# A decoder step whose late stages do their element-wise work on DVE alone, and whose epilogues write over the values they are given

## The chip, the cores and the metric

The kernel runs on one core of a Trainium2 chip. The metric is the device time of one execution in microseconds. Three runs of the kernel before took 1580.48, 1581.73 and 1584.48 us, the median is 1581.73 us.

Five engines work side by side: PE multiplies matrices, DVE (VectorE), ACT (ScalarE) and POOL (GpSimd) do element-wise work, and the queue of SP issues all the DMAs that are spoken of here. Each engine takes its instructions strictly in the order that is written for it; one that waits holds up all that stand behind it. All of POOL's work in this kernel has its operands in SBUF.

## The reference, cut to what matters

One layer: a wide input projection, two branches (a gated recurrence A and windowed attention B), each projected back, a merge with sigmoid gates, an output projection, a norm and a gated embedding that is added.

```python
    u = rmsnorm(x, norm_pre)
    proj = jnp.einsum('bld,de->ble', u, w_in)
    aq, af, ai, aog, az, bq, bk, bv, bz, ga, gb = jnp.split(proj, offs, axis=-1)
    ...
    oa = (oa * jax.nn.silu(az.astype(jnp.float32))).astype(x.dtype)
    a = jnp.einsum('ble,ed->bld', oa, w_pa)
    ...
    b = jnp.einsum('ble,ed->bld', ob, w_pb)
    m = jax.nn.sigmoid(ga) * a + jax.nn.sigmoid(gb) * b
    y = jnp.einsum('bld,de->ble', m, w_o)
    x = x + rmsnorm(y, norm_post)
    e = jnp.einsum('blp,pd->bld', pl, w_ple) * jax.nn.sigmoid(jnp.einsum('bld,de->ble', x, w_ple_gate))
    x = x + e
```

There are 1024 prompt tokens and 32 sample tokens (1056 columns), the model is 1024 wide, everything is float32.

## The kernel before, in words

Values lie transposed: 128 channels in the partitions, tokens in the columns, eight tiles of 128 x 1056 for a 1024-wide value. Each float32 operand of a matmul is split into a high part (`H..`, `wh`) and a low part (`L..`, `wl` = value - high); a product is three matmuls, high x high, high x low, low x high.

**A pair.** `pair_gemm` makes two output tiles (two times 128 channels) at once, with a Strassen-like scheme over the first three of each four k-tiles: seven products P1, P5, P6, P3, P7, P2, P4 (nine matmuls of 512 columns each), each of which takes one combination of weights (`prep`, lines 288 to 316: sums `ws` at L296 and L309, the high part at L285, the low part at L286) and one variant of the values (B11, T1, T2, B22, T3, B21, T4). The remaining k-tiles ("R") are done plainly, four times six matmuls, after P6, P3, P2 and P4. The 32 sample columns are done apart, on `gs`, after P1. Three PSUM banks go round; the outputs leave them through DVE: `p` at L492, and the three `out` sums of L448 in the order u (after P3), p (after P7) and c (after P2); the fourth output is read by the epilogue from PSUM. P2 needs the bank that L492 has read, P4 the bank that the sum with p has read.

**The late stages**, four pairs each: the second gate (`gate_b`, pairs 0 to 3, of which 2 and 3 are "late"), projection A (`pa`), projection B with the merge (`pb`), the output projection (`o`), then the small embedding projection `ple` with the residual beside it, and its gate. The values of a stage are made from the outputs of the stage before by `build`: 12 differences (L1481), 25 high parts by ACT (L1469, L1483) and 25 low parts (L1470, L1484). A variant can be rebuilt only when the last pair of the stage before has used it, so `build` runs along the last pair of one stage and the first pair of the next, in the order B11, T1, T2, B22, R, T3, B21, T4. The epilogues of `pb` and `o` do not begin before the whole of `build` has been written down.

**Who does what.** Before, POOL makes the sums `ws`, the low parts of P1, P2 and P4, the low parts of B11 and of every second tile of the others, one of the merge additions (L1545), and in the residual (`residual`, lines 1604 to 1664) half of the multiplications by the norm's factor (L1648) and half of the low parts (L1662). DVE does the rest.

**Order.** PE's order is the order in which the code is written: the generators (`build`, `turn_p`, `residual`) are stepped by `tick()` every three matmuls in the late stages, and what they emit stands there. The order of the other engines is made by a scheduler when the kernel is built. A tile pool hands out a buffer when its former user is done with it: `ct`, three buffers of 128 x 512, is used by `out`, the epilogues, T3 and T4 of `build` and by `turn_p`; `t12` is one buffer, which `build` holds for `ts` until the last low part of T4, if it uses it for that.

`turn_p` (L1562) loads nine pieces of the layer's embedding (L1566), turns each by two transposes on PE (`ppp`, L1570) and splits it into `pH` and `pL` for `ple`.

Of the kernel before, what the change touches and what calls it, by code (L numbers as in the profile page):

```python
# [11 lines left out]
F32 = mybir.dt.float32  # L12
# [4 lines left out]
ALU = mybir.AluOpType  # L17
# [3 lines left out]
P = 128  # L21
# [6 lines left out]
M = 3  # L28
# [93 lines left out]
def tile_decoder_step(ctx: ExitStack, tc: tile.TileContext, x_prompt, x_sample, state_hgrn, cache_k, cache_v,  # L122
# [70 lines left out]
    def enqueue(gen, delay=1, q=0):  # L193
        queues[q].append([gen, delay])
# [94 lines left out]
    def prep(W):  # L289

        a11, a21, a12, a22 = (W.raw[i][:, 0:M, j, :] for i in range(2) for j in range(2))
        shape = [P, M, P]

        def sums(a, b, op):
            s = wp.tile(shape, F32, name=tname("ws"), tag="ws", bufs=2)
            G.tensor_tensor(s, a, b, op=op)  # L296
            return s

        split(W, "P1", a11, G, shape, "w", 4)
        yield  # L300
# [8 lines left out]
        G.tensor_tensor(s2, a12, s2, op=ALU.subtract)  # L309
        split(W, "P3", s2, V, shape, "w", 4)  # L310
        yield
        split(W, "P7", s3, V, shape, "w", 4)
        yield
        split(W, "P2", a12, G, shape, "w", 4)
        yield
        split(W, "P4", a22, G, shape, "w", 4)
        yield

    def prep_plain(W):

        shape = [P, M, P]
        for n, (i, j) in enumerate(((0, 0), (1, 0), (0, 1), (1, 1))):
            split(W, (i, j), W.raw[i][:, 0:M, j, :], G if n % 2 else V, shape, "w", 4)
            if n == 1:
                rest(W)
            yield
# [6 lines left out]
    def rest(W):  # L333
        if R:
# [468 lines left out]
    def hgrn_proj(h, pairs, pre=()):  # L803
# [615 lines left out]
    def gate_b(p, late=False):  # L1419
        def ep_gb(i):  # L1420
            def ep_(ci, sl, ps):
                sg = ctile()[:, :ps.shape[-1]]
                S.activation(sg, ps, AF.Tanh, scale=0.5)
                V.tensor_scalar(sg, sg, 0.5, 0.5, op0=ALU.mult, op1=ALU.add)
                DM.dma_start(gb_d[i][:, sl], sg)
            return ep_

        pair_gemm(gb_pairs[p], u, (ep_gb(2 * p), ep_gb(2 * p + 1)), quantum=3 if late else A_QUANTUM, late=late)
# [25 lines left out]
    def build(x, prev, src):  # L1454

        ts = rt.tile([P, M, HT], F32, name=tname("ts"), tag="t12")
        for n in ("B11", "T1", "T2", "B22", "R", "T3", "B21", "T4"):
            yield until(("used", id(prev), n))
            if n == "B22":
                sample_side(x)  # L1460
                for i in range(KT):
                    V.tensor_copy(x.s[:, i, :], src[i][:, ssl])
                x.made.add("s")
            if n == "R":
                for sl in (H0, H1):
                    for kt in range(KT):
                        if kt % 4 >= M:
                            h, l = block(x, kt, sl.start, sl.stop)
                            S.copy(h, src[kt][:, sl])  # L1469
                            (V if kt < 4 else G).tensor_tensor(l, src[kt][:, sl], h, op=ALU.subtract)  # L1470
                            yield B_WAIT
                x.made.add(n)
                continue
            for i in range(M):
                a, b = src[i], src[4 + i]
                s = {"B11": a[:, H1], "B22": b[:, H0], "B21": b[:, H1], "T1": ts[:, i], "T2": ts[:, i]}.get(n)
                if s is None:
                    s = ctile()
                if n[0] == "T":
                    p, q = {"T1": (a[:, H0], a[:, H1]), "T2": (b[:, H0], s), "T3": (b[:, H0], a[:, H0]), "T4": (b[:, H1], ts[:, i])}[n]  # L1480
                    V.tensor_tensor(s, p, q, op=ALU.subtract)  # L1481
                h, l = (v[:, i] for v in x.v[n])
                S.copy(h, s)  # L1483
                (G if i == 1 or n == "B11" else V).tensor_tensor(l, s, h, op=ALU.subtract)  # L1484
# [49 lines left out]
    def eps_pb(i):  # L1534
        gbt = gl.tile([P, NTOK], F32, name=f"gbr{i}", tag=f"gl{i // 4}", bufs=2)
        DM.dma_start(gbt, gb_d[i])

        def ep_(ci, sl, ps):
            if ms[i] is None:
                while ("built", id(xb)) not in done:  # L1540
                    tick()
                ms[i] = staged(i, "m")
                DM.dma_start(ms[i], ma_d[i])
            V.tensor_tensor(gbt[:, sl], gbt[:, sl], ps, op=ALU.mult)
            (G if ci == HT else V).tensor_tensor(ms[i][:, sl], ms[i][:, sl], gbt[:, sl], op=ALU.add)  # L1545
# [14 lines left out]
    yT = [None] * KT  # L1560

    def turn_p():  # L1562
        for i in range(9):
            r = P if i < 8 else 32
            pt = ctile()[:, :256]
            DM.dma_start(pt[:r], p_prompt[0, 0, i * P:(i + 1) * P, :] if i < 8 else p_sample[0].rearrange("b t d -> (b t) d"))  # L1566
            yield 4
            b = fps.tile([P, 512], F32, name=f"ppp{i}", tag="xp", bufs=3)
# [27 lines left out]
    small = rt.tile([P, M * HT], F32, name="small", tag="t12")  # L1596
# [8 lines left out]
    def residual():  # L1605
# [39 lines left out]
                S.copy(rb_[:, lo:lo + w], b[:, :w])  # L1645
        yield 2
        for n, i in enumerate(order):
            (G if n % 2 else V).tensor_tensor(yT[i], yT[i], rb_, op=ALU.mult)  # L1648
            for hf in range(3):
                m, r = (4, P) if hf < 2 else (1, 32)  # L1650
                b = fps.tile([P, 512], F32, name=f"xtp{i}_{hf}", tag="xp", bufs=3)
# [3 lines left out]
                V.tensor_tensor(yT[i][:, sl], yT[i][:, sl], b[:, :sl.stop - sl.start], op=ALU.add)  # L1655
# [89 lines left out]
```

## Time and profile before

| | |
|---|---|
| runs | 1580.48, 1581.73, 1584.48 us |
| the profiled execution, own time | 1583.84 us |
| its span, first to last instruction | 1581.9 us |
| mean granted PE clock | 0.983 |
| late stages in it (from the third pair of the second gate) | 1081.9 us to the end |

The page gives the busy time of each engine over the span. The late stages are read pair by pair: a pair of seven products has the same 107 matmul instructions everywhere, so that a pair that waits for nothing shows what PE needs for it, and the length of the others what they lose. The order of time on one engine shows, in brackets, how long the engine stood idle before an instruction and what ended that; a row with "x2" is two instructions back to back.

### The profile page before, as it was taken

How to read it: one execution, taken by the hardware profiler on the slowest of the kernel's cores; microseconds unless marked ns; L12 is line 12 of the kernel's file. 1: busy time of each engine (PE TensorE's matmuls, PEld its weight loads, DVE VectorE, ACT ScalarE, POOL GpSimd, SP SyncE). 2: the span in 40 equal slices, each digit the busy share in tenths (PEclk: the TensorE clock that was granted, in tenths of full speed). 3: DMA queues.
4: the chain of work that ended last, by engine and by line, in shares of the span. 5: the costliest groups of instructions: out<-in, count | busy, mean ns of one | idle time of the engine just before them, and what ended most of it. 6: DMA issues, size and time to landing. Idle time of an engine off the chain costs nothing.

```text
span 1581.9 us, 27515 instructions
## 1 busy us (share of the span) xinstructions
PE 1499.7 (95%) x10013; PEld 1180.4 (75%) x10013; DVE 1053.3 (67%) x2240; ACT 729.8 (46%) x1881; POOL 630.1 (40%) x550
## 2 busy tenths in 40 slices
PE   8888999999999999999899999999999997998998
PEld 8767787878777777787677776777777775788776
DVE  7666858584858585763677777744957879547432
ACT  6234444445353545445555565543624433545422
POOL 1355444535354444455222222232736556224200
PEclk9999999999999999999999999999999998999999
DMA  5212131212121212213112111135463631223221
GB/s 182 67 30 81 41 97 41 73 52 82 55 83 55 77 60 63 75 50 94 40 48 51 47 48 51 56 113 206 147 210 122 214 100 35 60 62 93 80 80 55
DMA packets 198003, 129.54 MB, mean 82 GB/s; under 512 B 47075, under 2 KB 185500, under 8 KB 197852
## 3 DMA queue, kind: packets, MB, share of 16 engines
q1 hardware_dynamic: 197052, 127.54, 26.6%
q8 instruction: 79, 1.29, 0.3%
q14 instruction: 56, 0.46, 0.1%
q0 software_dynamic: 672, 0.18, 0.1%
q10 hardware_dynamic: 144, 0.07, 0.0%
HBM read 96.89 MB, written 31.88 MB: 81 GB/s over the span
## 4 chain that ended last, share of the span: by engine, by line
PE 66%; DVE 22%; issue 4%; ACT 3%; DMA 3%; POOL 2%; SPq 0%; DVEq 0%; ACTq 0%; POOLq 0%
PE g L404 47%; PE gs L386 3%; DVE ct L448 2%; PE po L1259 2%; DVE QE L938 2%; PE pt L1244 1%; PE g L835 1%; DVE wl L286 1%; DVE LT L1484 1%; PE gs L394 1%; PE d L1053 1%; PE lp L1212 1%; DVE stk L1397 1%; PE d L1055 1%; PE d L1015 1%
## 5 line engine op out<-in xcount | busy, mean ns | idle before, releaser
L286 POOL TENSOR_TENSOR wl<-raw,wh 128x384 fp32r<-128x384 f32 x150 | 169.6, 1134 | 359.5 <-ACT wh L285 345.5
L404 PE MATMUL g<-HT,wh 128*128 128x512 f32 x588 | 242.7, 413 | 16.7 <-DVE ct L448 12.9
L404 PE MATMUL g<-LT,wh 128*128 128x512 f32 x588 | 234.0, 398 | 0.9 <-POOL LT L1484 0.9
L404 PE MATMUL g<-HT,wl 128*128 128x512 f32 x588 | 234.4, 399 | 0.0
L404 PE MATMUL g<-HB,wh 128*128 128x512 f32 x522 | 214.6, 411 | 7.1 <-ACT p L441 5.2
L404 PE MATMUL g<-HB,wl 128*128 128x512 f32 x522 | 206.2, 395 | 0.0
L404 PE MATMUL g<-LB,wh 128*128 128x512 f32 x522 | 205.9, 395 | 0.0
L285 ACT CAST wh<-ws 128x384 fp32r<-128x384 f32 x184 | 93.8, 511 | 175.4 <-PE g L404 114.0
L404 PE MATMUL g<-HR,wrh 128*128 128x512 f32 x416 | 174.0, 418 | 0.0
L404 PE MATMUL g<-HR,wrl 128*128 128x512 f32 x416 | 166.0, 399 | 0.0
L286 DVE TENSOR_TENSOR wl<-ws,wh 128x384 fp32r<-128x384 f32 x184 | 128.6, 700 | 55.7 <-ACT wh L285 54.4
L404 PE MATMUL g<-LR,wrh 128*128 128x512 f32 x416 | 165.4, 398 | 0.0
L404 PEld LDWEIGHTS g<-HT,wh 128*128 128x128 f32 x588 | 111.4, 189 | 62.8 <-issue 16.6
L285 ACT CAST wh<-raw 128x384 fp32r<-128x384 f32 (+1 forms) x170 | 86.2, 510 | 142.0 <-PE g L404 129.0
L404 PEld LDWEIGHTS g<-HT,wl 128*128 128x128 f32 x588 | 111.5, 190 | 24.9 <-issue 0.9
L404 PEld LDWEIGHTS g<-LT,wh 128*128 128x128 f32 x588 | 111.6, 190 | 22.1 <-POOL LT L1484 1.2
L404 PEld LDWEIGHTS g<-HB,wh 128*128 128x128 f32 x522 | 98.7, 189 | 33.2 <-ACT p L441 6.1
L296 POOL TENSOR_TENSOR ws<-raw 128x384 f32<-128x384 f32 x46 | 51.6, 1122 | 168.4 <-DVE wl L286 168.4
L404 PEld LDWEIGHTS g<-HB,wl 128*128 128x128 f32 x522 | 98.6, 189 | 21.9 <-issue 0.5
L404 PEld LDWEIGHTS g<-LB,wh 128*128 128x128 f32 x522 | 99.0, 190 | 18.2 <-issue 0.7
L404 PEld LDWEIGHTS g<-HR,wrl 128*128 128x128 f32 x416 | 79.4, 191 | 17.8 <-issue 0.5
L404 PEld LDWEIGHTS g<-HR,wrh 128*128 128x128 f32 x416 | 80.2, 193 | 15.5 <-issue 0.7
(422 smaller groups left out, 3051.4 us busy)
## 6 DMA issues: line engine op xcount, KB each, us to landing
raw<-in_w_in_dram SPq DMA_DIRECT2D x116, 256.0 KB
raw<-in_w_in_dram SPq DMA_DIRECT2D x64, 128.0 KB
oa_d<-G SPq DMA_DIRECT2D x8, 528.0 KB
oar<-oa_d SPq DMA_DIRECT2D x8, 528.0 KB
sga<-ga_d SPq DMA_DIRECT2D x8, 528.0 KB
obr<-ob_d SPq DMA_DIRECT2D x8, 528.0 KB
ma_d<-sga SPq DMA_DIRECT2D x8, 528.0 KB
gbr<-gb_d SPq DMA_DIRECT2D x8, 528.0 KB
```

What stands on the lines that cost most here:

```text
L285: S.copy(h, x)
L286: eng.tensor_tensor(l, x, h, op=ALU.subtract)
L296: G.tensor_tensor(s, a, b, op=op)
L386: T.matmul(gs[r, :2 * P], xs[:, k, :], raws[k // 4][:, k % 4].rearrange("p j m -> p (j m)"), start=k < 4, stop=k >= 4, tile_position=(0, 3 ...
L394: T.matmul(gs[:, 256 + 32 * j:288 + 32 * j], part[:, P * j:P * j + P], cst[:, C_S32:C_S32 + 32], start=True, stop=True)
L404: T.matmul(ps, a, b, start=start, stop=stop, skip_group_check=True)
L448: V.tensor_tensor(dst, ps, other, op=ALU.add)
L835: T.matmul(ps, a[:, k, :], b, start=k == 0 and m == 0, stop=k == KT - 1 and m == 2)
L938: V.tensor_tensor(Q16[:, :, j, :], src, T44[:, :, 0:1].broadcast_to([P, 64, 4]), op=ALU.mult)
L1015: T.matmul(b[:, c * P:(c + 1) * P], kn[:, c, :], vn[:, c, :], start=True, stop=True)
L1053: T.matmul(o, att[:, c, :], vn[:, c, :], start=True, stop=c == 0)
L1259: T.matmul(po[r, lo:hi], vN[:, kb, r], pT[:, j, lo:hi], start=i == 0, stop=i == len(items) - 1, skip_group_check=True, tile_position=(0, 6 ...
```

## The change

From the third pair of the second gate on, POOL does none of the element-wise work: a one-element list `helper` names the engine of the weights' sums and low parts; it is POOL, and is set to DVE ahead of the late stages. In `build`, in the merge and in the residual DVE takes all that POOL did. The copies of the sample columns (`x.s`) go from DVE to ACT. `own(ps)` gives an epilogue its own value as the place to write to when that lies in SBUF, and a new `ct` buffer only for PSUM; `ga`, `gb` and `o` use it. T4 of `build` is made in `ts` again and no longer in `ct`. `turn_p` has a tile of its own, `pw`, with six places, in the buffer `t12`, and begins when `build` of the output projection's values has been written down, not after 30 ticks.

```diff
+    def own(ps):
+
+        return ctile()[:, :ps.shape[-1]] if ps.space == PSUM else ps
...
         def sums(a, b, op):
             s = wp.tile(shape, F32, name=tname("ws"), tag="ws", bufs=2)
-            G.tensor_tensor(s, a, b, op=op)
+            helper[0].tensor_tensor(s, a, b, op=op)
             return s
 
-        split(W, "P1", a11, G, shape, "w", 4)
+        split(W, "P1", a11, helper[0], shape, "w", 4)
...
-        G.tensor_tensor(s2, a12, s2, op=ALU.subtract)
+        helper[0].tensor_tensor(s2, a12, s2, op=ALU.subtract)
...
-        split(W, "P2", a12, G, shape, "w", 4)
+        split(W, "P2", a12, helper[0], shape, "w", 4)
         yield
-        split(W, "P4", a22, G, shape, "w", 4)
+        split(W, "P4", a22, helper[0], shape, "w", 4)
...
+    helper = [G]
     plan = []
...
         def ep_ga(ci, sl, ps):
-            sg = ctile()[:, :ps.shape[-1]]
+            sg = own(ps)
             S.activation(sg, ps, AF.Sigmoid)
...
-                sg = ctile()[:, :ps.shape[-1]]
+                sg = own(ps)
                 S.activation(sg, ps, AF.Tanh, scale=0.5)
                 V.tensor_scalar(sg, sg, 0.5, 0.5, op0=ALU.mult, op1=ALU.add)
                 DM.dma_start(gb_d[i][:, sl], sg)
...
-                    V.tensor_copy(x.s[:, i, :], src[i][:, ssl])
+                    S.copy(x.s[:, i, :], src[i][:, ssl])
...
-                            (V if kt < 4 else G).tensor_tensor(l, src[kt][:, sl], h, op=ALU.subtract)
+                            V.tensor_tensor(l, src[kt][:, sl], h, op=ALU.subtract)
...
                 if s is None:
-                    s = ctile()
+                    s = ts[:, i] if n == "T4" else ctile()
...
-                (G if i == 1 or n == "B11" else V).tensor_tensor(l, s, h, op=ALU.subtract)
+                V.tensor_tensor(l, s, h, op=ALU.subtract)
...
+    helper[0] = V
     oar = load_staged(oa_d, "oar")
     gate_b(2, True)
...
-            (G if ci == HT else V).tensor_tensor(ms[i][:, sl], ms[i][:, sl], gbt[:, sl], op=ALU.add)
+            V.tensor_tensor(ms[i][:, sl], ms[i][:, sl], gbt[:, sl], op=ALU.add)
...
     def turn_p():
+        yield until(("built", id(xm)))
+        pw = rt.tile([P, 6, 256], F32, name="pw", tag="t12")
         for i in range(9):
             r = P if i < 8 else 32
-            pt = ctile()[:, :256]
+            pt = pw[:, i % 6, :]
             DM.dma_start(pt[:r], p_prompt[0, 0, i * P:(i + 1) * P, :] if i < 8 else p_sample[0].rearrange("b t d -> (b t) d"))
...
-                sq = ctile()[:, :ps.shape[-1]]
+                sq = own(ps)
                 S.activation(sq, ps, AF.Square)
                 V.tensor_tensor(acc[:, sl], acc[:, sl], sq, op=ALU.add)
...
-    enqueue(turn_p(), 30)
+    enqueue(turn_p(), 1)
...
-            (G if n % 2 else V).tensor_tensor(yT[i], yT[i], rb_, op=ALU.mult)
+            V.tensor_tensor(yT[i], yT[i], rb_, op=ALU.mult)
...
-            V.tensor_copy(x1.s[:, i, :], yT[i][:, ssl])
+            S.copy(x1.s[:, i, :], yT[i][:, ssl])
...
-                (V if n % 2 else G).tensor_tensor(l, yT[i][:, sl], h, op=ALU.subtract)
+                V.tensor_tensor(l, yT[i][:, sl], h, op=ALU.subtract)
```

In the program of the change POOL has 153 rows less, DVE 113 more, ACT 29 more and SP 7 less (some rows stand for several instructions); up to about the third pair of the second gate DVE and POOL have the same rows as before. Three places carry the prediction. Line numbers of the change are four to eight higher than those of before: L448 is L453 there, L492 L497, L1481 L1487, L1484 L1489, L1570 L1578, L1648 L1656, L1655 L1663, L1662 L1670.

**The last pair of the second gate, DVE**, from its `p` (L492) to the sum with p, for which PE's P4 waits; `ts`, `HT`, `LT`, `HB`, `LB` are build's. Before:

```order
L492 TENSOR_TENSOR p_11854<-g_11891,p_11854 128x512
L1484 TENSOR_TENSOR LT_11920<-ts_11814,HT_11919 128x512
L1481 TENSOR_TENSOR ts_11814<-oar_11611,ts_11814 128x512
L1484 TENSOR_TENSOR LB_11964<-oar_11607,HB_11963 128x512
L448 TENSOR_TENSOR ct_11932<-g_11834,u_11889 128x512
L1484 TENSOR_TENSOR LT_11920<-ts_11814,HT_11919 128x512
L1484 TENSOR_TENSOR LB_11964<-oar_11611,HB_11963 128x512
L1424 TENSOR_SCALAR ct_11934<-ct_11934 128x512
L448 TENSOR_TENSOR ct_11967<-g_11803,p_11854 128x512
```

The change, on the same stretch:

```order
L497 TENSOR_TENSOR p_11838<-g_11875,p_11838 128x512
L290 TENSOR_TENSOR wl_11887<-raw_11652,wh_11886 128x384
L1489 TENSOR_TENSOR LT_11903<-ts_11798,HT_11902 128x512
L1487 TENSOR_TENSOR ts_11798<-oar_11596,ts_11798 128x512
L290 TENSOR_TENSOR wl_11922<-raw_11733,wh_11921 128x384
L1487 TENSOR_TENSOR ts_11798<-oar_11598,ts_11798 128x512
L453 TENSOR_TENSOR ct_11916<-g_11818,u_11873 128x512
L1489 TENSOR_TENSOR LT_11903<-ts_11798,HT_11902 128x512 x2
L1429 TENSOR_SCALAR ct_11916<-ct_11916 128x512
L1489 TENSOR_TENSOR LB_11947<-oar_11594,HB_11946 128x512
L453 TENSOR_TENSOR ct_11950<-g_11787,p_11838 128x512
```

POOL's rows of this place (low parts of `ts` and `oar`, sums and low parts of weights) now stand among DVE's own: between the sum with u and the sum with p there stand three low parts and a scalar operation, where there stood two low parts and the scalar operation.

**The first pair of the output projection, PE**, where the first transposes of the embedding stand. `g_13880` is the bank of P2 before:

```order
L404 MATMUL g_13712<-HT_13782,wh_13745 128x512
L404 MATMUL g_13712<-LT_13783,wh_13745 128x512
L404 MATMUL g_13712<-HT_13782,wl_13746 128x512
L404 MATMUL g_13880<-HB_13796,wh_13764 128x512
L404 MATMUL g_13880<-LB_13797,wh_13764 128x512
L404 MATMUL g_13880<-HB_13796,wl_13765 128x512
L1570 MATMUL ppp_13893<-cst,ct_13855 128x128 x2
L404 MATMUL g_13880<-HB_13796,wh_13764 128x512
L404 MATMUL g_13880<-LB_13797,wh_13764 128x512
```

In the change they stand between the last matmul of P3 and the plain part that follows it (`g_13719` is the bank of P5 and P3):

```order
L409 MATMUL g_13719<-HB_13604,wl_13692 128x512
L409 MATMUL g_13719<-HB_13604,wh_13691 128x512
L409 MATMUL g_13719<-LB_13605,wh_13691 128x512
L409 MATMUL g_13719<-HB_13604,wl_13692 128x512
L1578 MATMUL ppp_13823<-cst,pw 128x128 x2
L409 MATMUL g_13719<-HR_13674,wrh_13651 128x512
L409 MATMUL g_13719<-LR_13675,wrh_13651 128x512
L409 MATMUL g_13719<-HR_13674,wrl_13652 128x512
L409 MATMUL g_13719<-HR_13674,wrh_13651 128x512
```

The transposes have moved ahead by 18 matmuls of 512 columns (the plain part, P7 and three of P2), to the end of P3. What they read, `pw`, is loaded into the buffer that `ts` holds until the last low part of T4; on DVE that stands at this place in the change, ahead of the `p` of the same pair (L497):

```order
L1489 TENSOR_TENSOR LT_13756<-ct_13757,HT_13755 128x512
L1489 TENSOR_TENSOR LT_13756<-ct_13763,HT_13755 128x512
L1489 TENSOR_TENSOR LT_13756<-ct_13767,HT_13755 128x512
L1489 TENSOR_TENSOR LB_13772<-m_12954,HB_13771 128x512
L1489 TENSOR_TENSOR LB_13772<-m_13142,HB_13771 128x512
L1489 TENSOR_TENSOR LB_13772<-m_13330,HB_13771 128x512
L1487 TENSOR_TENSOR ts_13457<-m_12954,ts_13457 128x512
L1487 TENSOR_TENSOR ts_13457<-m_13142,ts_13457 128x512
L1487 TENSOR_TENSOR ts_13457<-m_13330,ts_13457 128x512
L1489 TENSOR_TENSOR LT_13780<-ts_13457,HT_13779 128x512 x3
L1597 TENSOR_TENSOR acc<-acc,ct_13795 128x32
L497 TENSOR_TENSOR p_13737<-g_13800,p_13737 128x512
```

Before, the pieces went into `ct` buffers, which T4 shared with them one by one; now the whole of build's work, three T3 low parts, three of B21, three differences and three low parts of T4, stands ahead of the load.

**The residual, DVE**, from the first multiplication by the norm's factor (`acc`) on; `y_13818` is the first tile, `y_14255` the third. Before:

```order
L1648 TENSOR_TENSOR y_13818<-y_13818,acc 128x1056
L286 TENSOR_TENSOR wl_14723<-raw_14643,wh_14722 128x256
L1648 TENSOR_TENSOR y_14255<-y_14255,acc 128x1056
L1655 TENSOR_TENSOR y_13818<-y_13818,xtp_0_14745 128x512
L1655 TENSOR_TENSOR y_13818<-y_13818,xtp_1_14751 128x512
L1655 TENSOR_TENSOR y_13818<-y_13818,xtp_2_14757 128x32
L286 TENSOR_TENSOR wl_14785<-raw_14643,wh_14784 128x256
```

and POOL's row of multiplications:

```order
L1648 TENSOR_TENSOR y_14039<-y_14039,acc 128x1056
L1648 TENSOR_TENSOR y_13821<-y_13821,acc 128x1056
L1648 TENSOR_TENSOR y_14260<-y_14260,acc 128x1056
L1648 TENSOR_TENSOR y_14447<-y_14447,acc 128x1056
L1662 TENSOR_TENSOR LT_14766<-y_13818,HT_14765 128x512
L1662 TENSOR_TENSOR LB_14770<-y_13818,HB_14769 128x512
```

The change (`y_13790` the first tile, `y_14017` the second, `y_14215` the third):

```order
L1656 TENSOR_TENSOR y_13790<-y_13790,acc 128x1056
L290 TENSOR_TENSOR wl_14677<-raw_14597,wh_14676 128x256
L1656 TENSOR_TENSOR y_14017<-y_14017,acc 128x1056
L1663 TENSOR_TENSOR y_13790<-y_13790,xtp_0_14699 128x512
L1663 TENSOR_TENSOR y_13790<-y_13790,xtp_1_14705 128x512
L1663 TENSOR_TENSOR y_13790<-y_13790,xtp_2_14711 128x32
L290 TENSOR_TENSOR wl_14739<-raw_14597,wh_14738 128x256
L1670 TENSOR_TENSOR LT_14720<-y_13790,HT_14719 128x512
L1656 TENSOR_TENSOR y_14215<-y_14215,acc 128x1056
L1670 TENSOR_TENSOR LB_14724<-y_13790,HB_14723 128x512
L1663 TENSOR_TENSOR y_14017<-y_14017,xtp_0_14761 128x512
```

The four multiplications of POOL now stand among DVE's rows, each one tile or two ahead of its use.

More of the change, by code (lines that the diff above doesn't have):

```diff
@@ L322, in prep_plain @@
         for n, (i, j) in enumerate(((0, 0), (1, 0), (0, 1), (1, 1))):
-            split(W, (i, j), W.raw[i][:, 0:M, j, :], G if n % 2 else V, shape, "w", 4)
+            split(W, (i, j), W.raw[i][:, 0:M, j, :], helper[0] if n % 2 else V, shape, "w", 4)
             if n == 1:
@@ L1476, in build @@
                 s = {"B11": a[:, H1], "B22": b[:, H0], "B21": b[:, H1], "T1": ts[:, i], "T2": ts[:, i]}.get(n)
+                h, l = (v[:, i] for v in x.v[n])
                 if s is None:
-                    s = ctile()
+                    s = ts[:, i] if n == "T4" else ctile()
                 if n[0] == "T":
@@ L1481, in build @@
                     V.tensor_tensor(s, p, q, op=ALU.subtract)
-                h, l = (v[:, i] for v in x.v[n])
                 S.copy(h, s)
-                (G if i == 1 or n == "B11" else V).tensor_tensor(l, s, h, op=ALU.subtract)
+                V.tensor_tensor(l, s, h, op=ALU.subtract)
                 if i < M - 1:
```

## The prediction, as it was put on record before the result

> **What bounds the kernel now.** The page comes first, for the engines' shares.
>
> ```profile
> span 1581.9 us, 27515 instructions
> PE 1499.7 (95%) x10013; PEld 1180.4 (75%) x10013; DVE 1053.3 (67%) x2240; ACT 729.8 (46%) x1881; POOL 630.1 (40%) x550
> ```
>
> PE is the bound over the whole, and the change leaves its work alone. What can be won is PE's idle time in the late stages, so next comes a table of stretches, one for each pair: `gate_b` 2 and 3, `pa` 0, `pa` 2 (as a measure), `pa` 3, `pb` 0, `pb` 3, `o` 0 and 1, and two short ones of 6 us.
>
> ```profile
> core 0: us, PE busy (x) PEld busy (x) DVE busy (x) ACT busy (x) POOL busy (x), PEclk, DMA share, GB/s
> 1081.93:1106.47 24.54, 21.79 (x109) 17.04 (x107) 9.38 (x18) 8.58 (x20) 7.07 (x7) 1.00 0.82 286
> 1106.47:1133.27 26.80, 23.34 (x109) 18.17 (x107) 23.81 (x36) 16.29 (x36) 19.29 (x14) 0.94 0.39 134
> 1133.27:1159.62 26.35, 23.86 (x108) 17.85 (x107) 25.34 (x32) 11.90 (x25) 15.15 (x12) 0.94 0.74 241
> ...
> 1181.30:1202.78 21.48, 21.48 (x108) 17.12 (x107) 8.60 (x16) 6.14 (x14) 7.33 (x7) 1.00 0.45 149
> 1202.78:1229.51 26.73, 23.36 (x109) 18.18 (x107) 24.70 (x34) 14.06 (x29) 20.13 (x14) 0.94 0.37 107
> 1229.51:1253.53 24.02, 22.36 (x109) 16.77 (x107) 23.88 (x33) 10.25 (x22) 14.34 (x12) 1.00 0.55 184
> ...
> 1296.49:1324.54 28.05, 23.69 (x109) 18.11 (x108) 27.03 (x38) 13.18 (x27) 19.16 (x15) 0.94 0.13 38
> 1324.54:1355.44 30.90, 25.78 (x115) 19.44 (x113) 27.88 (x32) 16.54 (x38) 19.41 (x14) 0.89 0.17 51
> 1355.44:1380.73 25.29, 23.32 (x120) 18.04 (x119) 12.29 (x24) 13.00 (x32) 7.03 (x7) 1.00 0.22 65
> ...
> 1338.40:1344.40 6.00, 6.00 (x14) 4.74 (x15) 6.00 (x7) 2.28 (x6) 4.12 (x4) 0.50 0.15 45
> 1447.80:1453.80 6.00, 6.00 (x23) 5.61 (x24) 6.00 (x6) 3.07 (x9) 5.34 (x3) 0.52 0.46 135
> ```
>
> A pair that waits for nothing takes 21.48 us. The pairs beside which `build` runs take 24.0 to 30.9, and in them DVE is busy nearly throughout (25.34 of 26.35, 27.03 of 28.05). The order of time on PE then names the waits:
>
> ```profile
> 1102.93 0.50 PE L404 MATMUL g<-HT,wh 128*128 128x512 f32 x1 [2.75 <-DVE ct L448]
> ...
> 1128.17 0.47 PE L404 MATMUL g<-HT,wh 128*128 128x512 f32 x1 [3.46 <-DVE ct L448]
> ...
> 1153.94 0.49 PE L404 MATMUL g<-HT,wh 128*128 128x512 f32 x1 [1.58 <-ACT HT L1483]
> 1155.29 0.50 PE L404 MATMUL g<-LT,wh 128*128 128x512 f32 x1 [0.85 <-POOL LT L1484]
> ...
> 1224.39 0.47 PE L404 MATMUL g<-HT,wh 128*128 128x512 f32 x1 [3.37 <-DVE ct L448]
> ...
> 1319.43 0.47 PE L404 MATMUL g<-HT,wh 128*128 128x512 f32 x1 [3.01 <-DVE ct L448]
> ...
> 1338.39 0.79 PE L404 MATMUL g<-HB,wh 128*128 128x512 f32 x1 [4.30 <-ACT p L441]
> ...
> 1369.52 0.41 PE L1570 MATMUL ppp<-cst,ct 128*128 128x128 f32 x2 [1.97 <-DMA ct<-in_p_prompt_dram]
> ...
> 1447.74 0.48 PE L1653 MATMUL xtp<-cst,xc 128*128 128x128 f32 x1 [4.76 <-DVE y L1655]
> ```
>
> Four are P4 waiting for the sum with p. Behind the longest waits stands a second loss: after 1338.39 and 1447.74 the granted clock is 0.50 and 0.52 for 6 us (the two last stretches), in which half of the matmuls' rate is gone, 3 us each. Why is DVE late? Its rows and POOL's:
>
> ```profile
> 1095.13 0.69 DVE L1481 TENSOR_TENSOR ts<-oar 128x512 f32<-128x512 f32 x1 [1.14 <-DMA oar<-oa_d]
> 1095.74 0.68 DVE L448 TENSOR_TENSOR ct<-g,u 128x512 f32<-128x512 f32 x1
> ...
> 1073.93 1.02 DVE L286 TENSOR_TENSOR wl<-ws,wh 128x384 fp32r<-128x384 f32 x2
> ...
> 1121.61 1.78 DVE L1481 TENSOR_TENSOR ts<-oar,ts 128x512 f32<-128x512 f32 x1
> ...
> 1087.89 1.01 POOL L286 TENSOR_TENSOR wl<-raw,wh 128x384 fp32r<-128x384 f32 x1 [11.11 <-ACT wh L285]
> ...
> 1121.09 1.75 POOL L1484 TENSOR_TENSOR LT<-ts,HT 128x512 fp32r<-128x512 f32 x1
> ```
>
> With POOL idle a 512-column operation of DVE is followed by the next after 0.61 us (1095.13 to 1095.74), and two of 384 take 1.02, so 0.47 each. Beside a POOL row the same L1481 takes 1.78. POOL saves DVE 0.61 and costs it 1.1.
>
> **The change part by part.** DVE gets POOL's rows (x14 in `gate_b` 3) at 0.47 or 0.61 and loses all its long ones. In `pa` 0 it has 32 + 12 = 44 rows: 44 x 0.47 = 20.7 at least, 44 x 0.61 = 26.8 at most, against 21.48 of PE: about full, so each wait must be looked at in the order. Times below count from the start of a pair on PE; at (21.48 - 1.6) / 87 = 0.2285 a matmul, with 1.6 for the sample parts, P3 and its plain part end at 12.6, P7 at 14.6, and P4 wants its bank at 18.0.
>
> `gate_b` 2: the `ct` buffers were held until DMAs had landed.
>
> ```profile
> 1099.89 1.00 POOL L309 TENSOR_TENSOR ws<-raw,ws 128x384 f32<-128x384 f32 x1 [0.99 <-DMA gb_d<-ct]
> ...
> 1102.18 0.69 DVE L448 TENSOR_TENSOR ct<-g,p 128x512 f32<-128x512 f32 x1 [2.38 <-DMA gb_d<-ct]
> ```
>
> One buffer was back by 1099.89, the other, for the second tile of the tanh, near 1102. Writing in place needs only the first: L448 at 1099.9, P4 0.7 late instead of 2.9: **-2.2**.
>
> `gate_b` 3: u is read from 12.6 on, then come three low parts and a scalar and p's sum (5 x 0.61 + 0.34 in all), out at 16.0, before 18.0. 26.80 becomes 21.7: **-5.1**. `pa` 3 likewise (u a little later, four rows between, out at 16.4): 26.73 to 21.6, **-5.1**. `pb` 3 has five rows between, two of them the merge's, and comes out at 17.4, still in time: 28.05 to 21.8, **-6.2**.
>
> `pa` 0: p's sum cannot start before 14.6; behind it come a low part and five more rows, so that T4's second low part is out at 19.4, its third at 20, P4 waits about 1.2: 22.7, **-3.6**.
>
> `pb` 0: P2 (14.6) waits for the `p` of L492, ahead of which stands all of `build` from R on. In the change that is 20 rows of 512 columns and 4 of 384, 14.1 us, begun at 1.6 (DVE's backlog); with `p` itself and a handover to ACT it ends at 16.9. PE waits 2.3: 23.8, **-0.2**.
>
> `o` 0 and 1: here the change adds a wait. The first `ppp` stands behind P3, 11.2 us into the pair, and reads `pw`, whose buffer `ts` holds until T4's last low part. From the last epilogue of `pb` to that low part DVE has 21 rows of 512 and 5 of 384, 21 x 0.61 + 5 x 0.47 = 15.2 us; with the 2.3 by which it is behind at the pair's start (six rows and a half of work after p's sum, less PE's end), 17.5. Then the load:
>
> ```profile
> 1366.44 0.97 SPq L1566 DMA_DIRECT2D ct<-in_p_prompt_dram  x2
> ```
>
> Its second DMA begins by 1367.1, PE goes on at 1369.52: 2.4 us. So PE stands from 11.2 to 19.9, 8.7 us, with everything queued behind the two transposes (the plain part, P7, P2); ACT and DVE have their own rows to go on with, and L492 is then no longer late. The clock's 3 us come on top. `o` 0: 21.48 + 1.5 (five `ppp`, by 1.8 for six in `o` 1: 25.29 - 1.97 - 21.48) + 8.7 + 3.0 = 34.7, not 30.90; `o` 1 loses its 1.97 and two `ppp`, 22.7, not 25.29: **+1.2** together. The bounds of this wait: 4 (DVE not behind, no clock) to 15 (T4 as late as before, 21.8 into the pair, and a longer cold spell).
>
> The Trainium skill, "TensorE: Matmul & The Clock Gate", section "What's actually happening", says that the clock halves after an idle window of about 3.4 us and is given back after a busy one of that length; by that the cold spell would cost 1.7 and not 3.0, and the sum would be 1.3 lower. The row above shows 6 us at 0.50, so the trace decides for 3.0.
>
> The residual, where PE waited 4.76 for L1655:
>
> ```profile
> 1437.38 12.00 POOL L1648 TENSOR_TENSOR y<-y,acc 128x1056 f32<-128x1056 f32 x4 [26.14 <-ACT acc L1645]
> ...
> 1437.59 3.52 DVE L1648 TENSOR_TENSOR y<-y,acc 128x1056 f32<-128x1056 f32 x1
> ...
> 1447.01 1.37 DVE L1655 TENSOR_TENSOR y<-y,xtp 128x512 f32<-128x512 f32 x3
> ```
>
> POOL's four L1648 keep DVE's two at 3.5 each. Alone, 1056 columns are two of 512 and a bit: 1.25. By the order of the change the first L1655 comes after two of these and a short row, 1437.6 + 2.9 = 1440.5, and PE reached its wait at 1443.0. Per tile DVE then has 1.25 + 1.37 + 1.22 = 3.8 us, PE about 4.1: it just keeps up. 4.76 and 3.0 of clock go, 0.8 may come back: **-7.0**.
>
> The eight copies per stage on ACT (busiest in `gate_b` 3, 16.29 of 26.80) and T4 in `ts` cost nothing as long as ACT has that room; without it some 1 us a stage.
>
> Sum: -2.2 - 5.1 - 5.1 - 6.2 - 3.6 - 0.2 + 1.2 - 7.0 = -28.2. I take 3.4 off for small waits that a full DVE will put in pairs that now have none: -24.8. The profiled execution took 1583.84 (its span and 1.94 around it), 2.1 over the median of 1581.73, so 1559.0 on its own scale and **1557** on the median's.
>
> **The rivals.**
> (a) DVE becomes the bound: with 44 rows per pair it never gets ahead, and each of the six pairs keeps 1.5 to 2.5 of its wait: 12 more, 1569. For it: 25.34 busy of 26.35. Against: the long rows are POOL's doing. The Trainium skill, "Perfetto Trace Analysis", section "Optimizing Scalar/DVE Operations", advises to offload work when DVE is saturated, even to GpSimd, and adds that the shared port may spoil it; by the advice alone this rival would hold, the row of 1.78 speaks for the addition.
> (b) The wait for `pw` is short, since DVE is not behind and the clock holds: 8 less, 1549.
> (c) Slower: DVE's long rows are not POOL's doing (but DMA's or ACT's traffic). Then DVE stays as long and gets POOL's work on top: in `pa` 0 25.34 + 12 x 0.55 = 31.9 of DVE work in 26.35, 5.6 more; with the six pairs' POOL rows (14 + 12 + 14 + 12 + 15 + 14 = 81) 45 us, less some 12 of slack: 1615. It decides if L1481 still takes over 1.2 on average. Against it: 1095.13 ran at 0.69 while DMA was at its fullest.
> (d) That POOL keeps the work is excluded by the order of the change.
>
> **How the numbers follow.** 0.61 for the forecast (1551 to 1565), 0.20 for (a), 0.13 for (b), 0.06 for (c). 1546 to 1571 takes in the forecast, (b) and most of (a). A difference under 0.3% (4.7 us, about what a measurement of this kernel can tell from no change) needs a time over 1577: the end of (a), 0.06. Faster 0.88, same 0.06, slower 0.06.
>
> **What would show it.** L1487 at 0.69 throughout; `gate_b` 3, `pa` 3 and `pb` 3 at about 21.6; no wait for L453; a wait of PE for the DMA of `pw` in `o` 0 of about 9 us, the pair at 33 to 36; the first L1663 before 1441 less what was won ahead of it. It is wrong if PE waits for low parts of weights, now on DVE, in pairs that ran at 21.48, or if the wait for `pw` is absent.

## The result, and the profile after

The kernel after takes 1553.82 us (median; 1553.37 to 1554.42) against 1581.73 (1580.48 to 1584.48): the ratio is 0.982, 95% interval [0.980, 0.984], 27.9 us less. The prediction said 1557, 24.7 less, within 1546 to 1571. The page's head shows that POOL has lost 200 us of work, DVE carries 124 instructions more and is busy no longer than before:

```profile
span 1551.2 us, 27351 instructions
PE 1484.1 (96%) x10013; PEld 1171.6 (76%) x10013; DVE 1054.1 (68%) x2364; ACT 736.3 (47%) x1913; POOL 430.5 (28%) x394
```

The table of stretches for the pairs that the prediction reckons with: `gate_b` 2 and 3, `pa` 0, `pa` 3, `pb` 0, `pb` 3, `o` 0 and 1; then the stretch from `o` 3 to the residual's end and the first pair of the last gate.

```profile
core 0: us, PE busy (x) PEld busy (x) DVE busy (x) ACT busy (x) POOL busy (x), PEclk, DMA share, GB/s
1080.28:1105.95 25.67, 23.28 (x108) 18.13 (x107) 13.24 (x26) 8.66 (x20) 0.00 (x0) 0.93 0.85 294
1105.95:1127.44 21.49, 21.49 (x109) 17.12 (x107) 18.61 (x36) 16.62 (x42) 0.00 (x0) 1.00 0.44 143
1127.44:1149.65 22.21, 21.80 (x109) 17.04 (x108) 21.79 (x43) 11.91 (x25) 0.00 (x0) 1.00 0.79 265
1192.60:1214.08 21.48, 21.48 (x108) 17.12 (x107) 18.78 (x35) 14.22 (x36) 0.00 (x0) 1.00 0.47 135
1214.08:1237.83 23.75, 21.81 (x108) 17.04 (x107) 23.41 (x46) 10.89 (x23) 0.00 (x0) 1.00 0.83 272
1280.80:1302.56 21.76, 21.74 (x108) 17.04 (x107) 20.00 (x39) 14.03 (x35) 0.00 (x0) 1.00 0.17 49
1302.56:1335.48 32.92, 24.55 (x118) 19.11 (x117) 27.12 (x51) 17.84 (x40) 0.00 (x0) 0.90 0.22 66
1335.48:1358.23 22.75, 22.75 (x118) 17.85 (x117) 13.66 (x29) 13.17 (x31) 0.00 (x0) 1.00 0.16 47
...
1379.71:1442.43 62.72, 62.72 (x369) 55.52 (x368) 41.67 (x92) 35.98 (x99) 0.00 (x0) 1.00 0.35 104
1442.43:1472.77 30.34, 28.84 (x153) 22.59 (x152) 16.42 (x32) 11.90 (x24) 0.00 (x0) 1.00 0.23 66
```

The stretch from `o` 3 to the residual's end before:

```profile
1402.21:1473.08 70.87, 65.90 (x370) 57.82 (x369) 45.26 (x85) 35.12 (x93) 24.88 (x14) 0.95 0.31 91
```

Three of the eight pairs now run at 21.5 to 21.8. In `gate_b` 3 DVE has as many rows as before (36) and is busy for 18.61 instead of 23.81. Three waits of PE stand out in the order of time:

```profile
1100.92 0.79 PE L409 MATMUL g<-HT,wh 128*128 128x512 f32 x1 [2.39 <-DVE ct L453]
...
1230.86 0.50 PE L409 MATMUL g<-HB,wh 128*128 128x512 f32 x1 [1.94 <-DVE p L497]
...
1322.38 0.69 PE L1578 MATMUL ppp<-cst,pw 128*128 128x128 f32 x2 [8.37 <-DMA pw<-in_p_prompt_dram]
```

The first was not forecast, the second (`pb` 0) and third (`pw`) were, at 2.3 and 8.7. None of DVE's long rows is left, as the view of the line L1487 shows; it gives least, median and greatest duration in ns:

```profile
L1487 DVE TENSOR_TENSOR ts<-oar,ts x6: 682/686/687, 1114.9 to 1145.2; 128x512 f32<-128x512 f32 x6
L1487 DVE TENSOR_TENSOR ct<-oar,oar x3: 684/686/687, 1131.7 to 1136.1; 128x512 f32<-128x512 f32 x3
```

Before, the same view tells more than the prediction had read from it:

```profile
L1481 DVE TENSOR_TENSOR ts<-oar,ts x3: 1387/1496/1779, 1114.7 to 1121.6; 128x512 f32<-128x512 f32 x3
```
```profile
L448 DVE TENSOR_TENSOR ct<-g,p x11: 676/680/692, 1102.2 to 1348.1; 128x512 f32<-128x512 f32 x11
```

Of the additions and subtractions (TENSOR_TENSOR), only those with both inputs in SBUF were stretched beside POOL. L448, which reads one input from PSUM (`g`), was never over 0.692 in all its rows. What was late before were the rows queued ahead of it. Copies and scalar operations with a single input, from SBUF, were stretched as well: a copy of 32 columns (L1462) took up to 1.33, where DVE without POOL (e1, below) takes 0.19 at most. For the scalar operation L1424 here are the group's busy time and mean (in ns) in the late stages before, where L1429 after has a mean of 425:

```profile
L1424 DVE TENSOR_SCALAR ct<-ct 128x512 f32<-128x512 f32 x8 | 5.2, 650 | 2.2 <-ACT ct L1423 2.2
```

### The profile page after: what moved, and what is told of

It is laid out like the page before. It is cut to its first block, busy times and chain, and to the rows that moved or that the text cites. A ratio compares the mean times of both kernels' runs of the same rounds, so it can differ in the third digit from the quotient of the medians.

```text
span 1551.2 us, 27351 instructions
## 1 busy us (share of the span) xinstructions
PE 1484.1 (96%) x10013; PEld 1171.6 (76%) x10013; DVE 1054.1 (68%) x2364; ACT 736.3 (47%) x1913; POOL 430.5 (28%) x394
## 4 chain that ended last, share of the span: by engine, by line
PE 71%; DVE 18%; issue 3%; ACT 3%; DMA 3%; POOL 1%; SPq 0%; DVEq 0%; ACTq 0%; POOLq 0%
PE g L409 51%; PE gs L391 3%; PE po L1264 2%; DVE ct L453 2%; PE g L1684 2%; DVE QE L943 2%; PE pt L1249 1%; PE g L840 1%; PE gs L399 1%; PE d L1058 1%; DVE wl L290 1%; PE lp L1217 1%; DVE stk L1402 1%; PE d L1060 1%; DMA raw<-in_w_in_dram 1%
## 5 line engine op out<-in xcount | busy, mean ns | idle before, releaser
L290 POOL TENSOR_TENSOR wl<-raw,wh 128x384 fp32r<-128x384 f32 x101 | 113.3, 1126 | 231.2 <-ACT wh L289 217.1
L290 DVE TENSOR_TENSOR wl<-ws,wh 128x384 fp32r<-128x384 f32 x184 | 122.2, 666 | 54.3 <-ACT wh L289 53.0
L409 PEld LDWEIGHTS g<-HT,wl 128*128 128x128 f32 x588 | 111.0, 189 | 24.8 <-issue 0.9
L409 PEld LDWEIGHTS g<-LT,wh 128*128 128x128 f32 x588 | 111.5, 190 | 21.5 <-DVE LT L1489 0.8
L409 PEld LDWEIGHTS g<-HB,wl 128*128 128x128 f32 x522 | 98.1, 188 | 21.6 <-issue 0.5
L409 PEld LDWEIGHTS g<-LR,wrh 128*128 128x128 f32 x416 | 79.0, 190 | 14.2 <-issue 0.7
```

The source lines that it names most:

```text
L290: eng.tensor_tensor(l, x, h, op=ALU.subtract)
L409: T.matmul(ps, a, b, start=start, stop=stop, skip_group_check=True)
```

## The experiments

Ratios are to the kernel before. In the four series of runs its median was 1581.7 (with the kernel after), 1582.4 (e1, e2, e5, e6), 1584.1 (e3, e4, e8, e9) and 1584.4 (e7, e10, e11, e12), so a difference of 2 or 3 us between medians of different series means little.

**Which part of the change wins.** e1 gives the kernel before nothing but DVE in place of POOL; e2 is the kernel after with all of POOL's rows given back; e5 and e6 give back the weights' rows alone, or the rest alone. The quoted texts are what was expected, in the order e1, e2, e5, e6.

```diff
 e1 (from before):
-            G.tensor_tensor(s, a, b, op=op)
+            helper[0].tensor_tensor(s, a, b, op=op)
...
-                (G if i == 1 or n == "B11" else V).tensor_tensor(l, s, h, op=ALU.subtract)
+                V.tensor_tensor(l, s, h, op=ALU.subtract)
...
 e5 (from after):
-    helper[0] = V
 e6 (from after):
-                V.tensor_tensor(l, s, h, op=ALU.subtract)
+                (G if i == 1 or n == "B11" else V).tensor_tensor(l, s, h, op=ALU.subtract)
...
 e2: e5 and e6
```

> The kernel before, with only POOL's late rows given to DVE (weights' sums and low parts, the builds' low parts, the merge, the residual); epilogues keep a second ct buffer, ppp keeps its data in ct, T4 stays in ct. Contention theory (POOL's rows and DVE's rows with two inputs in SBUF hold each other up): nearly the whole gain is here, and the 8.4 wait for pw with its cold clock is not: 1545 to 1553, DVE's L-row of the sums T2 at 0.69 throughout, PE in the third pair with build at 21.5. Rival (the buffers are what counts: in-place epilogues and pw): 1570 or more.

> The kernel after with all of POOL's rows given back to POOL: what is left of the change are the epilogues in place, pw, T4 in ts and the sample copies on ACT. Contention theory: no gain, rather a loss, since T4's last low part is as late as before and pw waits for it longer (21.8 into o 0 in place of 17.8): 1580 to 1592, wait of PE for the DMA of pw 11 to 14. Rival (buffers): 1565 or less.

> The kernel after with only the weights' sums and low parts back on POOL in the late stages (7 rows of 384 columns a pair); builds, merge and residual stay on DVE. Contention theory: DVE is relieved of 7 x 0.47 = 3.3 a pair, but each of the 7 POOL rows makes about one row of DVE 0.8 to 1.1 longer where a build runs: 1556 to 1564, waits for L453 back in gate_b 3, pa 3 and pb 3 at 0.5 to 2 each, pairs without build at 21.48. Rival (a full DVE is helped by any offload): faster than after, 1550 or less, pb 0 without its 1.9.

> The kernel after with the weights on DVE, but with the builds' low parts, the merge and the residual's rows divided between DVE and POOL as before. Contention theory: 5 to 8 POOL rows of 1.3 to 1.7 in each pair with build, and the residual's 4.8 wait and cold clock back: 1563 to 1575, of which 6 to 8 in the residual alone. Rival (any offload helps): 1552 or less in the pairs, with only the residual's 7 on top: 1559.

| | median us | ratio |
|---|---|---|
| e1 DVE alone | 1557.54 | 0.986 [0.984, 0.988] |
| e2 buffers alone | 1589.49 | 1.005 [1.004, 1.007] |
| e5 weights on POOL | 1571.70 | 0.994 [0.993, 0.996] |
| e6 builds on POOL | 1576.33 | 0.996 [0.994, 0.998] |

DVE alone is worth 24.8 of the 1582.4 that before took beside it; the buffers alone lose 7.1. The two do not add up: together they took 27.9 and not 17.7, so with POOL out of the way the buffers' edits lose nothing. e1 came out over its 1553: the wait for `pw` is indeed absent, but `o` 0 waits 3.6 for p's sum and `o` 1 waits 1.1 for the data in `ct`, and the stretch from `o` 3 to the end of the first gate pair takes 5.1 more than in the kernel after, 1.6 of it in waits and the rest at a lower clock (means of 0.85 to 0.96). What of e1's distance to 1553.82 belongs to the buffers and the copies on ACT, and what to the clock, isn't separated.

In e2 the wait for `pw` is 5.4 and not 11 to 14, since PE had already stood 4.3 for `p` in the same pair; together 9.6. e5 was priced too low: POOL's 8 rows in `pb` 0 take 17.04, 2.1 each, and the wait for L453 is 5.3; in `o` 0 T4 is so late that `pw` is waited for 13.7.

```profile
1215.61:1247.14 31.53, 24.09 (x108) 18.16 (x107) 24.48 (x43) 11.49 (x24) 17.04 (x8) 0.89 0.64 204
```

DVE is relieved of rows there (43 for 46) and is busy for longer (24.48 for 23.41). e6 ranged from 1569.6 to 1580.7, its median a little over what was expected; the residual's stretch is back at 70.90, and its old wait to the hundredth:

```profile
1437.49 0.69 PE L1661 MATMUL xtp<-cst,xc 128*128 128x128 f32 x2 [4.76 <-DVE y L1663]
```

None of the offloads to POOL helped.

**What it is in POOL's rows that costs DVE.** Idle POOL was given 12 dummy rows of 512 columns, once copies within SBUF (e10), once zeros (e11).

```diff
     acc = rt.tile([P, NTOK], F32, name="acc")
+    G.memset(acc, 0.0)
...
                     V.tensor_tensor(s, p, q, op=ALU.subtract)
+                if x is xb and n[0] == "T":
+                    G.tensor_copy(acc[:, 0:1], s[:, 0:1])
+                    G.tensor_copy(acc[:, 1:513], acc[:, 513:1025])
 e11, in place of the last line:
+                    G.memset(acc[:, 1:513], 0.0)
```

> The kernel after, with idle POOL given 12 dummy rows in pa 3 and pb 0: after each sum T of the build of xb it copies one column of that sum (so that it comes at that time) and then 512 columns of acc, SBUF to SBUF. The output is the reference's. Theory (a DVE row with both inputs in SBUF and a POOL row that reads SBUF hold each other up): rows of L1492 and L1494 in these two pairs lengthen from 0.69 to 1.2 to 1.8 in about one row for each copy, rows with an input in PSUM stay at 0.69; the two pairs grow from 45.2 by 3 to 8, 1557 to 1562. Rival (POOL's rows cost DVE nothing by themselves, the rest of the change made DVE's rows short): 0.69, 1553 to 1555.

> The same 12 places, but POOL fills the 512 columns with zeros instead of copying them: it writes SBUF and reads one column only. Theory (reading is what collides): DVE's rows at 0.69 throughout except beside the one-column copies, the pairs as in the kernel after, 1553 to 1555. Rival (any POOL row at work slows DVE): as with the copies, 1557 or more.

1557.15 with copies (0.983 [0.981, 0.984]), 1553.67 with zeros (0.981 [0.979, 0.982]). The scheduler moved the wide rows, which wait for nothing, to 1074 to 1085, ahead of the late stages, so `pa` 3 and `pb` 0 show nothing. But there they met other DVE rows. First the copies as the view of their line has them (least, median, greatest in ns), then DVE's rows beside them in order of time:

```profile
L1491 POOL COPY acc<-acc x12: 612/618/1802, 1075.1 to 1084.0; 128x512 f32<-128x512 f32 x12
```
```profile
1075.11 0.67 DVE L453 TENSOR_TENSOR ct<-g,c 128x512 f32<-128x512 f32 x1
...
1081.94 1.56 DVE L344 TENSOR_TENSOR wrl<-raw,wrh 128x256 fp32r<-128x256 f32 x2 [0.61 <-ACT wrh L343]
1083.42 0.83 DVE L1429 TENSOR_SCALAR ct<-ct 128x512 f32<-128x512 f32 x1
1084.18 0.95 DVE L290 TENSOR_TENSOR wl<-ws,wh 128x384 fp32r<-128x384 f32 x1
```

The same two views of the run with zeros; POOL is at them until 1081.0, so that the last two rows are DVE's almost by itself:

```profile
L1491 POOL MEMSET acc<- x12: 526/527/720, 1073.9 to 1080.5; 128x512 f32 x12
```
```profile
1074.55 0.53 DVE L300 TENSOR_TENSOR ws<-raw 128x384 f32<-128x384 f32 x1
...
1079.52 0.56 DVE L290 TENSOR_TENSOR wl<-ws,wh 128x384 fp32r<-128x384 f32 x1 [0.79 <-ACT wh L289]
1080.80 0.76 DVE L344 TENSOR_TENSOR wrl<-raw,wrh 128x256 fp32r<-128x256 f32 x2 [0.72 <-ACT wrh L343]
1081.60 0.43 DVE L1429 TENSOR_SCALAR ct<-ct 128x512 f32<-128x512 f32 x1
```

Beside copies the two L344 take 1.56 together, not 0.76, and a 384-column row (L290) 0.95; beside zeros it takes its bare 0.56, and L300 0.53. One copy in its turn took 1.80 and not 0.62, and one of the one-column copies in `pb` 0 took 2.93, another only 0.18: either side can be the one that is held up. The Trainium skill, "SBUF — State Buffer", section "Who interferes with whom", states this: a DVE instruction with two SBUF inputs contends with a GpSimd instruction that reads SBUF, not with one that only writes, and one with at most one SBUF input does not, unless it runs in a two-port mode, which tensor_scalar can enter. The traces agree on each of these: L448 and L453, with one input from PSUM, are unchanged beside POOL's reads, and L1429, a tensor_scalar, takes 0.83 beside copies and 0.43 by itself (in which mode it ran the traces do not say). What such copies would cost in `pa` 3 and `pb` 0 was not measured, and the whole times decide little. Of the 4.7 by which e10's profiled execution is longer than e11's, 1.2 lie ahead of the copies and 2.4 in slower clock behind waits that both have (`gate_b` 2, `pb` 0); the other 1.1 lie in `gate_b` 2, where PE waits 3.73 for L453 in the one and 2.63 in the other. It is the length of the rows that shows the collision.

**The three waits that are left.**

```diff
 e3:
         yield until(("built", id(xm)))
+        yield 30
 e4:
-                sg = own(ps)
+                sg = acc[:, 32 * i:32 * i + 32] if late and ci == NP else own(ps)
 e8:
-            if late:
-                V.tensor_tensor(p5, b, p5, op=ALU.add)
-            else:
-                t = ctile()
-                S.copy(t, b)
-                G.tensor_tensor(p5, p5, t, op=ALU.add)
+            t = ctile()
+            S.copy(t, b)
+            (V if late else G).tensor_tensor(p5, p5, t, op=ALU.add)
 e9: e3, e4 and e8. e7: e3 and e4. e12: e3, e4 and
-        for n in ("B11", "T1", "T2", "B22", "R", "T3", "B21", "T4"):
+        for n in ("B11", "T1", "T2", "B22", "T3", "B21", "R", "T4"):
```

What was expected of e3, e4, e8, e9, e7 and e12, in this order:

> The kernel after, with turn_p waiting 30 more ticks (90 matmuls) once xm is built, so that the ppp transposes stand in o 1 and o 2. Theory: the wait for pw (8.4) goes and its cold clock with it, but DVE is still late with p's sum, whose wait the longer one had hidden: L497 ended 17.8 into o 0, P2 wants its bank at 14.6, so 3.4 of wait stay. o 0 24.9 to 26.4, o 1 about 22.8, together 7 less: 1546 to 1548. Rival A (as the prediction said, nothing else is late): o 0 at 22, 1543. Rival B (the transposes take their wait along): 1552 or more.

> The kernel after, with the tanh of the 32 sample columns in gate_b 2 and 3 written to acc, which is free there, instead of a ct buffer. Theory: gate_b 2 waits for L453 because two ct buffers hold these 32 columns until their DMAs land behind the eight loads of oar; without that the pair takes 21.5 to 22.2 in place of 25.7 (2.4 of wait, 1.4 of cold clock, 0.4 of filling): 1550. Rival (the third ct buffer, or the next load, is as late): gate_b 2 at 24 or more, 1552 to 1554.

> The kernel after, with the plain part of tile 1 copied out of its bank by ACT into a ct buffer and added to p by DVE from there, in the late pairs as in the earlier ones, so that P2's bank no longer waits for DVE's queue. Theory: pb 0 loses its 1.9 and pa 0 its 0.4, the wait for pw stays: 1551 to 1552. Rival (DVE's sum comes as late as before, P4 waits for it instead, and the ct buffer is missing elsewhere): 1554 to 1558.

> The three edits of e3, e4 and e8 together in the kernel after. Theory: they add up, and ACT's copy also takes the 3.4 that e3 leaves in o 0: 1538 to 1542, pairs of gate_b, pa, pb and o all at 21.5 to 23. Rival (DVE is full in pb 0 and o 0 whatever the order): 1545 or more, P4 waiting for L453 in pb 0 and o 0.

> The kernel after with the later ppp and the sample columns in acc, p's sum by DVE as in the kernel after. Theory: the two add up, 5.3 and 3.9 less than 1553.8: 1544 to 1545, the waits of P2 for p's sum (1.9 in pb 0, 3.6 in o 0) still there, each with or without a cold spell of 1.5. Rival: 1542.8 or less, ACT's copy is worth nothing.

> The same, and the builds make T3 and B21 ahead of R instead of behind it: both are free before the last pair of the stage before has ended, R only at its end. Theory (P2 waits because all of build from R on stands ahead of p's sum in DVE's queue at the start of pa 0, pb 0 and o 0): 9 of its rows, 5.5 us, move into the pair before, and the waits of 0.4, 1.9 and 3.6 go with their cold spells; pb 0 and o 0 at 21.5 to 22: 1536 to 1539. Rival (the pair before has no room for them, p's sum is late there): 1543 or more, L453 waited for in gate_b 3, pa 3 or pb 3.

| | median us | ratio |
|---|---|---|
| e3 later `ppp` | 1548.52 | 0.978 [0.977, 0.980] |
| e4 sample columns in `acc` | 1549.89 | 0.979 [0.978, 0.980] |
| e8 p by way of ACT | 1553.91 | 0.982 [0.980, 0.983] |
| e9 all three | 1542.77 | 0.974 [0.973, 0.976] |
| e7 e3 and e4 | 1546.48 | 0.976 [0.974, 0.977] |
| e12 e7 and the other order | 1544.24 | 0.975 [0.973, 0.976] |

e4 came out as expected; e3 and e7 lie 0.5 and 1.5 over their ranges, e9 0.8; e8 lies between its theory and its rival. e12 took the time of its rival, but not in the rival's way: L453 was waited for only 0.3, in `pb` 3.

e4 settles `gate_b` 2: the pair drops from 25.67 to the bare 21.48 with the load of `oar` at full strength beside it (DMA share 0.84).

```profile
1081.70:1103.18 21.48, 21.48 (x108) 17.11 (x107) 12.90 (x26) 8.58 (x20) 0.00 (x0) 1.00 0.84 291
```

e3 takes the wait for `pw` away and uncovers what it had hidden, in `o` 0:

```profile
1303.04:1330.04 27.00, 23.39 (x109) 18.18 (x107) 25.35 (x47) 16.22 (x36) 0.00 (x0) 0.94 0.23 69
```
```profile
1321.50 0.50 PE L409 MATMUL g<-HB,wh 128*128 128x512 f32 x1 [3.62 <-DVE p L497]
```

e8, e9 and e12 then try to get round DVE's queue, and the wait moves: with ACT's copy it stands at P4 in `pb` 0 (1.5 in place of 1.9), with R last it stands at R's low part, 1.3 in `pb` 0 and 3.6 in `o` 0.

```profile
1209.30:1232.68 23.38, 22.05 (x108) 17.03 (x107) 23.01 (x45) 10.41 (x23) 0.00 (x0) 1.00 0.82 275
...
1297.71:1325.54 27.83, 24.26 (x109) 18.95 (x108) 25.25 (x47) 16.31 (x36) 0.00 (x0) 0.88 0.22 67
```
```profile
1309.51 0.80 PE L409 MATMUL g<-LR,wrh 128*128 128x512 f32 x1 [3.57 <-DVE LR L1475]
```

The reason stands in the DVE column: 23.0 of 23.4 in `pb` 0, 25.3 of 27.8 in `o` 0, where PE alone needs 21.5. In `pb` 0 DVE is the bound, and another order only says who waits. In `o` 0 DVE's rows alone take more than 21.5 as well; some of the rest is slow clock (0.88), and e9 had this pair at 25.7. e9 has the lowest median, 1542.77, 11 less than the kernel after; 7.3 of that are e3 and e4 by e7's median. The intervals of e7, e9 and e12 overlap, so whether ACT's copy or the other order adds anything to e3 and e4 isn't decided; the copy alone gains nothing that can be measured.

## Why the prediction was right, step by step

All on the profiled executions, with spans of 1581.9 and 1551.2; times as after, in us.

| step | forecast | measured |
|---|---|---|
| `gate_b` 2 | 22.3 | 25.67 |
| `gate_b` 3 | 21.7 | 21.49 |
| `pa` 0 | 22.7 | 22.21 |
| `pa` 3 | 21.6 | 21.48 |
| `pb` 0 | 23.8 | 23.75 |
| `pb` 3 | 21.8 | 21.76 |
| `o` 0 + `o` 1 | 57.4 | 55.67 |
| residual's stretch | 63.9 | 62.72 |
| small waits elsewhere | +3.4 | none in the 21.48 pairs |

**The main reason held**, and the runs show it: DVE's long rows were POOL's doing, L1487 is at 0.69 throughout and up to 1.50 and 1.79 again where e5 and e6 give rows back, and in `pa` 0 DVE did 43 rows in 21.79, where it had taken 25.34 for 32. Rival (c) falls with it; so does (b), since the wait for `pw` was as long as forecast. Rival (a) is true in two places that the sum already held: `pb` 0 (DVE 23.41 of 23.75), and `o` 0, where it was covered. **`gate_b` 3, `pa` 0, `pa` 3, `pb` 0 and `pb` 3** came out within 0.5.

**`gate_b` 2 was the step that failed** within the sum: -2.2 was forecast, +1.1 came. "One buffer was back by 1099.89" was read from the bracket of a POOL row that uses no `ct` at all. The row that did use the buffer stands a little further down in the trace of before:

```profile
1101.95 0.63 ACT L1423 ACTIVATE ct<-ct 128x512 f32<-128x512 f32 x1 [2.73 <-DMA gb_d<-ct]
```

So both buffers, with the 32 sample columns of two tiles in them, came back near 1102, when their DMAs had got through behind the eight loads of `oar`. Writing in place needs one of them all the same. PE waited 2.4 as it had 2.75, and a cold spell on top of it, which before had not followed, made the 1.1. Of the prediction's signs, "no wait for L453" failed here and nowhere else.

**`o` 0**: the wait for `pw` was sized at 8.7 and measured 8.37, for the reason given (21 DVE rows up to T4's last low part). That "L492 is then no longer late" was right only under its cover (e3). The clock was mis-sized: 3.0 was put in from the row of before, and the matmuls behind 1322.38 show

```profile
1322.38:1325.38 3.00, 3.00 (x8) 2.48 (x9) 0.98 (x2) 0.37 (x1) 0.00 (x0) 0.50 0.94 284
1325.38:1328.38 3.00, 3.00 (x14) 2.42 (x13) 1.15 (x3) 1.93 (x4) 0.00 (x0) 0.90 0.32 108
```

Half speed until about 1325.9, seven matmuls at 0.43 instead of 0.23, 1.5 in all. The Trainium skill, "TensorE: Matmul & The Clock Gate", section "What's actually happening", which the prediction turned down, was nearer here: its window of about 3.4 us gives an estimate of 1.7. Its condition, an idle window of that length, is not what the traces show: spells followed waits of 2.39 in `gate_b` 2 and 1.94 in e3's `pb` 0.

**The residual** gained 8.15 where 7.0 was forecast. That is all that this stretch had lost: 4.97 of idle PE and 3.18 of slow clock. The 0.8 set aside for DVE's keeping up was not needed, and POOL's rows there were the whole wait (e6 brought it back). 0.5 came back in the first gate pair, 30.34 for 29.83, where PE now waits 0.85 for the sample columns' copy on ACT.

**The allowance of 3.4** was wrong: no pair that ran at 21.48 lost anything. That it nearly cancels the 3.3 that `gate_b` 2 was short of is luck. The eight steps together took 28.8, against 24.8 with the allowance; the 4.0 between them are mostly `o` (1.7), the residual (1.2) and `pa` 0 (0.5), all better than forecast. A further 1.65 of the two spans' difference arose ahead of the late stages, no more than executions of one order differ by (see the last section); the medians hold 27.9.

## What to carry to other kernels

Where DVE and POOL both read SBUF at one time, price the DVE rows with two SBUF inputs at their stretched length before dividing work: here each half of the work given back to POOL cost 18 and 23 us, and DVE alone was busy no longer with all of it. Before a wait is credited, find the row that uses the very buffer, not a neighbour's bracket. And when a wait goes, look in the same pair for the next one in the queue: of the 9.9 us that `pw` and its cold clock cost, 5.3 could be had, by the medians.

## What the hardware showed that was not expected

The clock's cold spell does not follow from a wait's length. After 2.75 in `gate_b` 2 before there was none, after 2.39 in the kernel after there was one; the stretches behind the two waits:

```profile
1102.93:1106.47 3.54, 3.54 (x16) 2.92 (x16) 1.59 (x4) 1.58 (x4) 0.00 (x0) 1.00 0.72 244
```
```profile
1100.92:1103.92 3.00, 3.00 (x7) 2.42 (x8) 1.39 (x3) 1.21 (x2) 0.00 (x0) 0.50 0.71 266
```

Up to `o` the order of e3 is that of the kernel after. Yet `gate_b` 2 begins at 1078.72 there and at 1080.28 in the kernel after, and `pb` 0, where PE waits 1.94 in both, took 23.75 at a clock of 1.00 in the one and 25.35 at 0.93 in the other. Both pairs in e3's table of stretches:

```profile
1078.72:1105.04 26.32, 23.39 (x108) 18.16 (x107) 13.26 (x26) 8.74 (x20) 0.00 (x0) 0.94 0.84 287
...
1213.22:1238.57 25.35, 23.41 (x108) 18.21 (x107) 24.43 (x47) 10.90 (x23) 0.00 (x0) 0.93 0.85 264
```

In e1 a spell began with no wait, 1.4 us behind 18 matmuls of one column each, which keep PE occupied by the record and give it little to do:

```profile
1403.08 1.99 PE L1629 MATMUL sqp<-small,acc 128*128 128x1 f32 x18
```
```profile
1406.50:1409.50 3.00, 3.00 (x12) 3.00 (x11) 2.34 (x13) 1.06 (x5) 0.00 (x0) 0.50 0.00 0
```

That these two are cause and effect is not shown; in the kernel after the same 18 were followed by none. Whether a wait is followed by a spell of 1.5 us thus differs from execution to execution. Most of the 1.65 above comes of it: at 768 us PE waits alike in both kernels (3.35 before, 3.32 after), and the next 6.5 us ran at 0.55 before and at 0.74 after, which gives 32 matmul instructions in the one and 38 in the other. The kernel after was 0.46 ahead at the first row behind this wait and is 1.50 ahead at the same matmul some 5 us later (774.55 and 773.05). In e3 and e4, whose edits touch nothing ahead of `gate_b` 2, that pair begins at 1078.72 and 1081.70.

```profile
768.50:775.00 6.50, 6.50 (x32) 3.92 (x33) 4.21 (x14) 3.30 (x13) 0.00 (x0) 0.55 0.04 10
```
```profile
768.04:774.54 6.50, 6.50 (x38) 3.60 (x40) 4.91 (x15) 3.82 (x13) 0.00 (x0) 0.74 0.21 49
```
